# Putting the two halves of an adaLN modulation block into different column quarters of the array

## The chip, the cores and the metric

One core of one Trainium2 chip runs the whole step in one launch. The metric is the device time of the core in microseconds; the kernel before has a median of 1109.49 us over three runs (1108.55 to 1110.03).

Engines in the profile: PE is the matrix engine, PEld its weight loads, DVE the vector engine, ACT the scalar engine, POOL the GpSimd engine, SP the queue that issues the transfers.

## The reference, cut to what matters

Two layers act on 640 tokens of width 1024. Each layer normalizes its input, shifts and scales it by values made from a conditioning vector (adaLN), runs one mixer (a conformer convolution in layer 0, a bidirectional Mamba-2 SSD scan in layer 1), and adds the result, multiplied by a gate. What the change touches is this:

```python
def adaln_params(cond, w, b):
    m = jax.nn.silu(cond) @ w + b          # cond: width 1024, w: 1024 x 3072
    return jnp.split(m, 3, axis=-1)        # shift, scale, gate
...
u = h @ w_in + b_in                        # conformer branch of layer 0
a, a_gate, z = jnp.split(u, 3, axis=-1)
v = a * jax.nn.sigmoid(a_gate)
v = depthwise_conv(v, w_dw, b_dw)          # 31 taps
v = jax.nn.silu(layer_norm(v, ln_g, ln_b))
return (v * jax.nn.silu(z)) @ w_out
```

There are two conditions, one for the 128 context tokens and one for the 512 sample tokens, so each product with `w` has only two rows that count.

## The kernel before, in words

**The big products.** Activations lie with channels on the partitions and tokens along the free axis. A weight comes by DMA as f32 (`wf`), ACT casts its high part to fp32r (`wh`), and DVE or POOL subtracts to get the low part (`wl`). A product is then three: `h_hi` with `wh`, `h_hi` with `wl`, `h_lo` with `wh` (`dense`, L148, and `product`, L499). The trace shows these as 128x320 products.

**The modulation blocks.** 3072 columns of two layers make 24 blocks of 256 columns; the two halves of a block are 128 columns each, for instance shift and scale of one channel tile. For a block, `ada_products` multiplies the conditions (`scz[:, k, :]`, 128 x 32, two columns that count) with eight weight tiles of 128 x 256. The stationary operand is 32 columns wide, so the four column quarters of the array hold four weight tiles at a time: tile k goes to quarter k % 4, and the result in PSUM has four groups of 32 rows that must still be added. `row` is a copy of that to SBUF (ACT). `ada_turn` multiplies it by a constant of zeros and ones, `sel`, which adds the quarters and turns the result so that channels lie on partitions: one product for each half. `ada_bias` (DVE, L129) adds the bias and writes `mod`. In the trace one f32 product has two weight loads and two product records.

**Where the blocks run.** Eight blocks stand at the start (`ada(k)`), between norm of the input, its modulation (`h_hi` and `h_lo`, L214 and L219) and the first products of layer 0, `u`. A tile scheduler orders them there by its own costs. Twelve stand in the loop of layer 0, one in each of twelve channel tiles: `lead` (L582) puts the sixteen products ahead of the gate tile's own product, `after_g` (L516) copies the row, the turn stands behind the tile of `a` (L596), and `after_a` adds the bias. The order in this loop comes from a planner that is given costs in us with each step: `op(ACT, 0.36, ...)` for the row copy, `op(PE, 0.25, ...)` for the turn. Four more blocks stand ahead of layer 1 (`gates`), again ordered by the tile scheduler. These use PSUM named `ada`; in the loop the rows lie in spare columns of the `u` tiles.

**The rest of layer 0.** The depthwise convolution runs on DVE (`cva`, L633, one instruction a tap) and, for other taps, on ACT (`tp`, L664) with POOL adding (`cv`, L705). Then comes a norm over channels: sums on PE (`pst`, `pmr`), then for each of sixteen tiles `cn` minus mean (L805), times the reciprocal (L806), silu on ACT (L807), and times `sz` (L811) on DVE. ACT and POOL make `y_hi` and `y_lo` of it, and PE multiplies with `w_out` into the `o` tiles (L148), whose low weight parts `wl` (L80) are made on DVE between the norm's instructions.

Of the kernel before, what the change touches and what calls it, by code (L numbers as in the profile page):

```python
# [7 lines left out]
F32 = mybir.dt.float32  # L8
# [5 lines left out]
P = 128  # L14
NT = 640
NP = 128
HN = 320
KD = 8
# [8 lines left out]
_n = 0  # L27
for _name, _w in (
    ("ng0", 8), ("ng1", 8), ("fg", 8), ("ada_b", 48), ("cond", 16), ("w_c", 24 * 5), ("b_c", 24),
    ("sn_g", 16), ("dtb", 1), ("alog", 1), ("sel", 2), ("eye", 128), ("d", 32),  # L30
):
    _C[_name] = (_n, _n + _w)
    _n += _w
# [8 lines left out]
def trunk(ctx: ExitStack, tc: tile.TileContext, a: dict):  # L42
# [5 lines left out]
    V, S, G, T = nc.vector, nc.scalar, nc.gpsimd, nc.tensor  # L48
# [6 lines left out]
    def c(name, i=0, n=1):  # L55
        o = _C[name][0] + i
        if o >= NCST:
            return cst0[0][:, o - NCST : o - NCST + n]
        return cst[:, o : o + n]

    eye = c("eye", 0, 128)
# [45 lines left out]

    def ada_products(ws, ps, busy=None):
        for k, w in enumerate(ws):
            q = k % 4 * 32  # L110
            T.matmul(ps[q : q + 32, 0:256], lhsT=scz[:, k, :], rhs=w, start=k < 4, stop=k >= 4)
            if busy is not None and k % 4 == 3:

                for b in range(2):
                    T.matmul(busy[:, b, 0:256], lhsT=w[:, 0:128], rhs=w, start=True, stop=True)
        row = ap.tile([P, 256], F32, tag="ada_row", bufs=2, name="ada_row")
        S.copy(out=row, in_=ps[:, 0:256])
        return row

    def ada_turn(row, ps):  # L120
        for j in range(2):
            T.matmul(ps[:, 2 * j : 2 * j + 2], lhsT=row[:, j * 128 : j * 128 + 128], rhs=c("sel", 0, 2), start=True, stop=True)

    def ada_bias(l, b, ps, act=False):
        if act:
# [109 lines left out]
    PE, ACT, VE, PO, SP, VL = range(6)  # L235
# [95 lines left out]
    def op(eng, dur, fn, table=None):  # L331
        return "op", ((eng, dur, fn, table),)
# [71 lines left out]
    with tc.tile_pool(name="l0", bufs=1) as lp:  # L404
# [102 lines left out]
        def after_g(i, ps, n=None):  # L507

            yield get("tm")
            sgs[i] = tmp.tile([P, NT], F32, tag="tm", bufs=2, name="sg")  # L510
            t = yield op(ACT, 0.79, lambda: S.activation(out=halves(sgs[i]), in_=ps[:, :, 0:HN], func=AF.Sigmoid, bias=c("b_in", 16 + i)), "sig")
            post(("sg", i), t)
            if n is not None:
                l, b, ws = rows_[n][0]
                r = ap.tile([P, 256], F32, tag="ada_row", bufs=2, name="ada_row")
                t = yield op(ACT, 0.36, lambda: S.copy(out=r.rearrange("p (b n) -> p b n", b=2), in_=ps[:, :, HN : HN + 128]))  # L516
                rows_[n] = l, b, r
                post(("row", n), t)
            if i != 1:
                put("mm", t)  # L520
# [48 lines left out]
        def filler():  # L569
            for name in plan:  # L570
                i = int(name[1:])
                n = i - 2 if 2 <= i < 14 else None
                if name[0] == "g":
                    lead = None
                    if n is not None:
                        yield key(("wa", n))

                        def lead(ps):
                            for k, w in enumerate(rows_[n][0][2]):
                                q = k % 4 * 32  # L580
                                for b in range(2):
                                    T.matmul(ps[q : q + 32, b, HN : HN + 128], lhsT=scz[:, k, :], rhs=w[:, b * 128 : b * 128 + 128], start=k < 4, stop=k >= 4)  # L582
                    ps, t = yield from product(16 + i, lead)
                    if n is not None:
                        for _ in range(4):
                            put("cs", t)
                        post(("ada", n), t)
                    start(after_g(i, ps, n), t)
                elif name[0] == "z":
                    ps, t = yield from product(32 + i)  # L590
                    start(after_z(i, ps), t)
                else:
                    ps, t = yield from product(i)
                    if n is not None:
                        yield key(("row", n))
                        t = yield op(PE, 0.25, lambda: ada_turn(rows_[n][2], ps[:, 0, 480:484]))  # L596
                    j = i - 6 if i >= 6 else None
                    if j is not None:
                        yield key(("sq", j))

                        def sums():
                            for t_, b in ((cv[j], 0), (sgs["sq", j], 1)):
                                quarter_sums(ps[:, b, HN : HN + QN], t_, True, True)
                        t = yield op(PE, 0.78, sums)
                        put("tm", t)
                    start(after_a(i, ps, n, j), t)
# [1139 lines left out]
def layout(inp):  # L1746

    import numpy as np

    f = {k: np.asarray(v) for k, v in inp.items()}  # L1750
    con = np.ascontiguousarray
    z = {}
    xa = np.concatenate([f["x_prompt"].reshape(2, 64, 1024), f["x_sample"].reshape(2, 256, 1024)], axis=1)
    z["x"] = con(xa.reshape(NT, KD, P).transpose(2, 1, 0))
    blocks = [(k, 8 + k) for k in range(8)] + [(16 + 2 * k, 17 + 2 * k) for k in range(4)]
    wa = f["ada_w"].reshape(2, KD, P, 24, 128)
    z["w_ada"] = con(np.stack([wa[:, :, :, list(b)] for b in blocks], axis=1).transpose(0, 1, 3, 2, 4, 5)).reshape(24, P, 2048)
    z["w_in1"] = con(f["conv_w_in"][0].reshape(KD, P, 48, 128).transpose(2, 1, 0, 3)).reshape(48, P, 1024)
    wo = f["conv_w_out"][0].reshape(8, 2, P, 1024)
    for i, (m0, nm) in enumerate(((0, 2), (2, 4), (6, 2))):  # L1760
        z[f"w_out1_{i}"] = con(wo[:, :, :, m0 * 128 : (m0 + nm) * 128].transpose(0, 2, 1, 3)).reshape(8, P, 2 * nm * 128)
    wi = f["ssd_w_in"][0]
    z["w_xbc"] = con(wi[:, 2048:5120].reshape(KD, P, 24, 128).transpose(2, 1, 0, 3)).reshape(24, P, 1024)
    z["w_z"] = con(wi[:, 0:2048].reshape(KD, P, 16, 128).transpose(2, 1, 0, 3)).reshape(16, P, 1024)

    def rows4(v):

        return np.concatenate([v[0:32], v[0:32], v[32:64], v[32:64]])

    wd = rows4(wi[:, 5120:5184].T).T.reshape(KD, P, 128)  # L1770
    z["w_dt"] = con(wd.transpose(1, 0, 2)).reshape(P, 1024)
    z["w_out2"] = con(f["ssd_w_out"][0].reshape(4, 4, P, 4, 256).transpose(0, 3, 2, 1, 4)).reshape(4, 4, P, 1024)
    for k, n in (("st_f", "state_fwd"), ("st_b", "state_bwd")):
        z[k] = con(f[n][0, 0].reshape(NG, 8, 64, 128).transpose(0, 3, 1, 2)).reshape(NG, P, 512)
    cs = np.zeros((P, NCST + NCST0), np.float32)

    def put(name, arr):
        lo, hi = _C[name]
        cs[: arr.shape[0], lo:hi] = arr

    def cols(v):
        return v.reshape(-1, P).T

    put("ng0", cols(f["norm_g"][0]))
    put("ng1", cols(f["norm_g"][1]))
    put("fg", cols(f["final_norm_g"]))
    put("b_in", cols(f["conv_b_in"][0]))
    put("w_dw", f["conv_w_dw"][0].reshape(CK, 16, P).transpose(2, 1, 0).reshape(P, 16 * CK))
    put("b_dw", cols(f["conv_b_dw"][0]))
    put("ln_g", cols(f["conv_ln_g"][0]))  # L1790
    put("ln_b", cols(f["conv_ln_b"][0]))
    put("ada_b", np.stack([f["ada_b"].reshape(2, 24, P)[:, list(b)] for b in blocks], axis=1).reshape(48, P).T)
    put("cond", np.stack([f["c_ctx"].reshape(KD, P).T, f["c"][0].reshape(KD, P).T], axis=-1).reshape(P, 16))
    put("w_c", f["ssd_w_conv"][0].reshape(5, 24, P).transpose(2, 1, 0).reshape(P, 120))
    put("b_c", cols(f["ssd_b_conv"][0]))
    put("sn_g", cols(f["ssd_norm_g"][0]))
    put("dtb", rows4(np.concatenate([f["ssd_dt_bias_f"][0], f["ssd_dt_bias_b"][0]]))[:, None])
    put("alog", rows4(np.concatenate([f["ssd_a_log_f"][0], f["ssd_a_log_b"][0]]))[:, None])
    sel = np.zeros((P, 2), np.float32)
    for q in range(0, P, 32):  # L1800
        sel[q, 0] = sel[q + 1, 1] = 1.0
    put("sel", sel)
    put("eye", np.eye(P, dtype=np.float32))
    put("d", np.broadcast_to(f["ssd_d"][0][None, :], (P, NH)))
    z["cst"] = cs
    lower = np.tril(np.ones((64, 64), np.int32), -1)
    z["msk"] = np.concatenate([lower, 1 - lower])
    return z
# [33 lines left out]
```

## Time and profile before

| what | value |
|---|---|
| median of the runs | 1109.49 us |
| lowest and highest run | 1108.55 and 1110.03 us |
| span of the profiled execution | 1108.6 us |
| PE busy | 1064.6 us (96%) |
| DVE busy | 815.5 us (74%) |
| ACT busy | 593.3 us (54%) |
| POOL busy | 521.2 us (47%) |

The span is that of one execution, and the median lies 0.9 us above it. The busy time of PE is modelled from its instruction stream. The modulation products of the start and of the stage ahead of layer 1 have line L111 (192 product records for 12 blocks), those of the loop L582 (384 records for 12 blocks), the turns L122, the row copies L117 and L516. Roughly, 0 to 64 us is the start, 64 to 316 the loop, 393 to 460 the norm with the first `o` products, 460 to 549 the other `o` products, 549 to 560 the stage ahead of layer 1, and the rest is layer 1.

### The profile page before, as it was taken

The numbers are of one execution on the slowest core, as the hardware profiler recorded it, in microseconds if no ns is written. First come the engines' busy times: TensorE is split into PE (matmuls) and PEld (weight loads), VectorE is DVE, ScalarE is ACT, GpSimd is POOL, SyncE is SP. The second block draws the span as 40 slices with busy tenths as digits, with TensorE's granted clock in tenths as the row PEclk, the third lists the DMA queues.
The fourth block names the chain that finished last, engine by engine and source line by source line (L and its number), as shares of the span: only waits on it lengthen the run. The fifth ranks groups of instructions, "written<-read, shape, count | busy, mean of one in ns | idle before, by whom it ended". The sixth has DMA issues, their size and how long they took to land.

```text
span 1108.6 us, 19536 instructions
## 1 busy us (share of the span) xinstructions
PE 1064.6 (96%) x7752; PEld 983.9 (89%) x7752; DVE 815.5 (74%) x1156; ACT 593.3 (54%) x1021; POOL 521.2 (47%) x447
## 2 busy tenths in 40 slices
PE   6999899999988999899999999999999999999996
PEld 3899899999987999899999887899889888978896
DVE  2589989999888479413369878988775786767673
ACT  6646565656665466312267657594536473743442
POOL 1059998988999647200000065413541443244213
PEclk9999999999989999899999999999999999999997
DMA  9364244332112111523402373424342514343102
GB/s 360 152 210 134 78 133 134 121 128 76 59 58 77 58 39 38 184 73 95 137 8 96 97 165 105 102 81 124 90 111 95 115 59 113 106 122 97 40 20 95
DMA packets 79051, 115.98 MB, mean 105 GB/s; under 512 B 26096, under 2 KB 49008, under 8 KB 78960
## 3 DMA queue, kind: packets, MB, share of 16 engines
q1 hardware_dynamic: 78240, 113.91, 34.3%
q8 instruction: 61, 1.00, 0.4%
q10 hardware_dynamic: 720, 0.82, 0.2%
q14 instruction: 30, 0.25, 0.1%
HBM read 109.80 MB, written 4.92 MB: 103 GB/s over the span
## 4 chain that ended last, share of the span: by engine, by line
PE 56%; DVE 21%; POOL 11%; ACT 5%; issue 4%; DMA 2%; SPq 0%; POOLq 0%; DVEq 0%; ACTq 0%
DVE cva L633 9%; PE pz L1004 8%; PE o L1004 8%; POOL cv L705 6%; PE xs L1004 6%; PE o L1513 3%; PE po L1285 2%; POOL wl L480 2%; PE pst L1222 2%; DVE cn L805 2%; PE B L1004 2%; PE py L1353 2%; DVE xs L1046 2%; PE o__5063 L148 1%; PE o__5065 L148 1%
## 5 line engine op out<-in xcount | busy, mean ns | idle before, releaser
L633 DVE SCALAR_TENSOR_TENSOR cva<-v,cst,cva 128x570 f32<-128x570 f32 (+10 forms) x359 | 276.2, 819 | 15.8 <-ACT cva L625 11.6
L705 POOL TENSOR_TENSOR cv<-cv,tp 128x490 f32<-128x490 f32 (+5 forms) x121 | 144.6, 1195 | 8.1
L664 ACT ACTIVATE tp<-v,cst 128x490 f32<-128x490 f32 (+5 forms) x121 | 85.6, 722 | 83.5 <-POOL cv L705 83.3
L966 ACT CAST wh<-wf 128x1024 fp32r<-128x1024 f32 x53 | 55.5, 1047 | 84.8 <-PE xs L1004 21.2
L480 POOL TENSOR_TENSOR wl<-wf,wh 128x1024 fp32r<-128x1024 f32 x37 | 89.0, 2405 | 14.6 <-ACT wh L477 11.0
L1004 PE MATMUL o<-yhl,wh 128*128 128x320 f32 x384 | 92.1, 327 | 0.0
L970 DVE TENSOR_TENSOR wl<-wf,wh 128x1024 fp32r<-128x1024 f32 x51 | 67.1, 1316 | 33.4 <-ACT wh L966 32.2
L1004 PE MATMUL pz<-h_hi,wh 128*128 128x384 f32 (+1 forms) x256 | 84.6, 330 | 0.5 <-ACT up L1033 0.5
L1291 POOL TENSOR_TENSOR y<-y,yo 128x512 f32<-128x512 f32 x32 | 44.6, 1395 | 79.8 <-DVE yo L1289 79.7
L1004 PE MATMUL pz<-h_hi,wl 128*128 128x384 f32 (+1 forms) x256 | 79.1, 309 | 0.0
L1004 PE MATMUL pz<-h_lo,wh 128*128 128x384 f32 (+1 forms) x256 | 79.0, 309 | 0.0
L1004 PE MATMUL xs<-h_hi,wh 128*128 128x384 f32 (+1 forms) x224 | 77.5, 346 | 0.0
L80 DVE TENSOR_TENSOR wl<-wf,wh 128x512 fp32r<-128x512 f32 (+1 forms) x25 | 26.3, 1054 | 69.3 <-ACT wh L78 69.3
L78 ACT CAST wh<-wf 128x1024 fp32r<-128x1024 f32 (+1 forms) x37 | 31.8, 860 | 83.9 <-PE o__5066 L148 39.2
L1004 PEld LDWEIGHTS o<-yhl,wh 128*128 128x128 f32 x384 | 63.9, 188 | 7.8 <-issue 7.8
L1046 DVE SCALAR_TENSOR_TENSOR xs<-up,cst,xs 128x642 f32<-128x642 f32 x64 | 68.3, 1069 | 2.6 <-ACT xs L1044 1.2
L1004 PE MATMUL xs<-h_hi,wl 128*128 128x384 f32 (+1 forms) x224 | 69.2, 309 | 0.0
L1004 PE MATMUL xs<-h_lo,wh 128*128 128x384 f32 (+1 forms) x224 | 69.1, 309 | 0.0
L1160 POOL TENSOR_TENSOR gb<-gb,cols 128x512 f32<-128x512 f32 x20 | 25.4, 1270 | 77.2 <-DMA gb<-acd 77.1
L1004 PE MATMUL o<-yhl,wl 128*128 128x320 f32 x192 | 59.2, 309 | 0.0
L1166 ACT ACTIVATE gf<-gf,cols 128x128 f32<-128x128 f32 x160 | 49.8, 390 | 16.2 <-DVE gf L1162 16.1
L909 POOL MEMSET up<- 128x2 f32 x2 | 0.2, 100 | 120.6 <-DVE h_lo L219 120.6
(764 smaller groups left out, 3487.1 us busy)
## 6 DMA issues: line engine op xcount, KB each, us to landing
wf<-w_in SPq DMA_DIRECT2D x48, 512.0 KB, 3.6
wa<-w_ada SPq DMA_DIRECT2D x64, 256.0 KB, 4.7
wf<-w_out SPq DMA_DIRECT2D x24, 512.0 KB, 4.0
wf<-w_xbc SPq DMA_DIRECT2D x24, 512.0 KB, 3.7
gf<-acd SPq DMA_DIRECT2D x40, 256.0 KB, 5.4
wa<-w_ada SPq DMA_DIRECT2D x16, 512.0 KB, 10.2
wf<-w_z SPq DMA_DIRECT2D x16, 512.0 KB, 3.9
gb<-acd SPq DMA_DIRECT2D x40, 128.0 KB, 4.6
```

Of the source, the lines that this page charges most:

```text
L78: S.copy(out=wh[:, :n], in_=wf[:, :n])
L480: t = yield either((PO, 2.41, lambda: G.tensor_sub(out=wl, in0=wf, in1=wh.bitcast(F32))), (VL, 1.23, lambda: V.tensor_sub(out=wl, in0=wf, ...
L633: t = yield op(VE, 0.24 + 0.01 * (hi - lo), lambda: V.scalar_tensor_tensor(out=rows64(accs[i], lo, hi), in0=rows64(vs[i], lo + d, hi + d), ...
L664: t = yield op(ACT, 0.72, lambda: S.activation(out=tp[:, :, 0 : hi - lo], in_=rows64(vs[i], lo + d, hi + d), func=AF.Copy, scale=w_dw(i, t ...
L705: t = yield op(PO, 1.12 if i < 14 else 1.3, lambda: G.tensor_add(out=rows64(cv[i], lo, hi), in0=rows64(cv[i], lo, hi), in1=sgs["tp", i, n] ...
L966: S.copy(out=cell["wh"], in_=cell["wf"])
L970: e_.tensor_sub(out=cell["wl"], in0=cell["wf"], in1=cell["wh"].bitcast(F32))
L1004: T.matmul(ps[:, b, at_ : at_ + t1 - t0], lhsT=w_, rhs=t_[:, t0:t1], start=k == 0 and n == 0, stop=k == nk - 1 and n == 2)
L1046: t = yield op(VL, 0.89, lambda: V.scalar_tensor_tensor(out=acc, in0=u[:, d : d + PW], scalar=c("w_c", j * 5 + d), in1=acc, op0=ALU.mult, ...
L1166: t = yield op(ACT, 0.39, lambda: S.activation(out=gv[:, h_, :], in_=gv[:, h_, :], func=AF.Exp, bias=cols1[ch][:, o8 + h_ : o8 + h_ + 1]), ...
L1291: t = yield op(PO, 1.29, lambda: G.tensor_add(out=y, in0=y, in1=yo))
L1513: T.matmul(ps, lhsT=wt, rhs=t_[:, tok], start=k == 0 and n == 0, stop=k == 3 and n == 2)
```

## The change

Half j of weight tile k goes to quarter `64 * j + k % 2 * 32` instead of both halves to quarter `k % 4 * 32`. A block is then sixteen products of 128 moving columns everywhere (in the loop it was that already), its result is 128 rows by 128 columns, the row copy is 128 wide instead of 256, and one turn with a `sel` of four columns takes the place of two turns with two. Two planner costs are lowered accordingly.

```diff
     def ada_products(ws, ps, busy=None):
         for k, w in enumerate(ws):
-            q = k % 4 * 32
-            T.matmul(ps[q : q + 32, 0:256], lhsT=scz[:, k, :], rhs=w, start=k < 4, stop=k >= 4)
+            for j in range(2):
+                q = 64 * j + k % 2 * 32
+                T.matmul(ps[q : q + 32, 0:128], lhsT=scz[:, k, :], rhs=w[:, j * 128 : j * 128 + 128], start=k < 2, stop=k >= KD - 2)
...
-        row = ap.tile([P, 256], F32, tag="ada_row", bufs=2, name="ada_row")
-        S.copy(out=row, in_=ps[:, 0:256])
+        row = ap.tile([P, P], F32, tag="ada_row", bufs=2, name="ada_row")
+        S.copy(out=row, in_=ps[:, 0:128])
         return row
 
     def ada_turn(row, ps):
-        for j in range(2):
-            T.matmul(ps[:, 2 * j : 2 * j + 2], lhsT=row[:, j * 128 : j * 128 + 128], rhs=c("sel", 0, 2), start=True, stop=True)
+        T.matmul(ps, lhsT=row, rhs=c("sel", 0, 4), start=True, stop=True)
...
-                r = ap.tile([P, 256], F32, tag="ada_row", bufs=2, name="ada_row")
-                t = yield op(ACT, 0.36, lambda: S.copy(out=r.rearrange("p (b n) -> p b n", b=2), in_=ps[:, :, HN : HN + 128]))
+                r = ap.tile([P, P], F32, tag="ada_row", bufs=2, name="ada_row")
+                t = yield op(ACT, 0.26, lambda: S.copy(out=r, in_=ps[:, 0, HN : HN + 128]))
...
                             for k, w in enumerate(rows_[n][0][2]):
-                                q = k % 4 * 32
                                 for b in range(2):
-                                    T.matmul(ps[q : q + 32, b, HN : HN + 128], lhsT=scz[:, k, :], rhs=w[:, b * 128 : b * 128 + 128], start=k < 4, stop=k >= 4)
+                                    q = 64 * b + k % 2 * 32
+                                    T.matmul(ps[q : q + 32, 0, HN : HN + 128], lhsT=scz[:, k, :], rhs=w[:, b * 128 : b * 128 + 128], start=k < 2, stop=k >= KD - 2)
...
-                        t = yield op(PE, 0.25, lambda: ada_turn(rows_[n][2], ps[:, 0, 480:484]))
+                        t = yield op(PE, 0.22, lambda: ada_turn(rows_[n][2], ps[:, 0, 480:484]))
...
-    sel = np.zeros((P, 2), np.float32)
+    sel = np.zeros((P, 4), np.float32)
     for q in range(0, P, 32):
-        sel[q, 0] = sel[q + 1, 1] = 1.0
+        for cd in range(2):
+            sel[q + cd, q // 64 * 2 + cd] = 1.0
```

In the loop of layer 0 the rows of PE stand as before, but for the turn, and on DVE, ACT and POOL a few neighbours change places. In the parts that the tile scheduler orders, more moves. On PE in the start, where `u__254` and the like are the first tiles of layer 0, the rows of before between 35 and 38 us of its trace are these (an L111 row of four products is half a block):

```order
L148 MATMUL u__254<-h_hi,wh 128x320
L122 MATMUL ada<-cst,ada_row 128x2 x2
L111 MATMUL ada<-wa,scz 32x256 x4
L148 MATMUL u__253<-h_lo,wh 128x320 x2
L111 MATMUL ada<-wa,scz 32x256 x4
L148 MATMUL u__102<-h_lo,wh 128x320 x2
L148 MATMUL u__254<-h_hi,wh 128x320
L148 MATMUL u__254<-h_hi,wl 128x320 x2
L148 MATMUL u__254<-h_lo,wh 128x320 x2
L111 MATMUL ada<-wa,scz 32x256 x8
```

From the turn at 34.54 us of the trace to the end of the last modulation products of the start, before has five groups of L111 with 4, 4, 8, 12 and 4 products. On PE at the end of that stretch the changed kernel has this (half a block is now eight products):

```order
L148 MATMUL u__274<-h_lo,wh 128x320 x2
L112 MATMUL ada<-wa,scz 32x128 x5
L122 MATMUL ada<-cst,ada_row 128x4
L112 MATMUL ada<-wa,scz 32x128 x3
L148 MATMUL u__102<-h_lo,wh 128x320
L112 MATMUL ada<-wa,scz 32x128 x8
L148 MATMUL u__102<-h_lo,wh 128x320
L148 MATMUL u__275<-h_lo,wh 128x320 x2
```

The same four blocks now stand in ten groups, of 8, 8, 8, 5, 3, 5, 11, 5, 3 and 8 products, and three of the turns stand inside a half block.

On DVE at the end of the norm, where the low weight parts `wl` for `w_out` stand between the norm's tiles, before has this:

```order
L811 TENSOR_TENSOR sz_4474<-cn,sz_4474 128x640
L80 TENSOR_TENSOR wl<-wf,wh 128x512
L805 TENSOR_TENSOR cn<-cv_3678,mu 128x640
L806 TENSOR_TENSOR cn<-cn,rl 128x640
L811 TENSOR_TENSOR sz_4544<-cn,sz_4544 128x640
L80 TENSOR_TENSOR wl<-wf,wh 128x512
L805 TENSOR_TENSOR cn<-cv_3857,mu 128x640
L806 TENSOR_TENSOR cn<-cn,rl 128x640
L811 TENSOR_TENSOR sz_4619<-cn,sz_4619 128x640
L80 TENSOR_TENSOR wl<-wf,wh 128x512
L811 TENSOR_TENSOR sz_4688<-cn,sz_4688 128x640
```

and the changed kernel, on the same engine and for the same tiles, this:

```order
L811 TENSOR_TENSOR sz_4518<-cn,sz_4518 128x640
L805 TENSOR_TENSOR cn<-cv_3722,mu 128x640
L806 TENSOR_TENSOR cn<-cn,rl 128x640
L811 TENSOR_TENSOR sz_4588<-cn,sz_4588 128x640
L80 TENSOR_TENSOR wl<-wf,wh 128x512
L805 TENSOR_TENSOR cn<-cv_3901,mu 128x640
L80 TENSOR_TENSOR wl<-wf,wh 128x512
L806 TENSOR_TENSOR cn<-cn,rl 128x640
L811 TENSOR_TENSOR sz_4663<-cn,sz_4663 128x640
L80 TENSOR_TENSOR wl<-wf,wh 128x512
L811 TENSOR_TENSOR sz_4732<-cn,sz_4732 128x640
```

The first of these three `wl` stands behind three more instructions of the norm than before, and the second stands ahead of two that it followed.

Layer 1 behind the stage of `gates` stands in the same order on every engine, and so do the transfers.

More of the change, by code (lines that the diff above doesn't have):

```diff
@@ L29 @@
     ("ng0", 8), ("ng1", 8), ("fg", 8), ("ada_b", 48), ("cond", 16), ("w_c", 24 * 5), ("b_c", 24),
-    ("sn_g", 16), ("dtb", 1), ("alog", 1), ("sel", 2), ("eye", 128), ("d", 32),
+    ("sn_g", 16), ("dtb", 1), ("alog", 1), ("sel", 4), ("eye", 128), ("d", 32),
 ):
```

## The prediction

> **What bounds the kernel now.** I read the page's busy line and chain first, then busy times by stage, then the chain and the waits inside the stage that holds half of the changed blocks, and last single rows of the weight loads where the changed work stands.
>
> ```profile
> PE 1064.6 (96%) x7752; PEld 983.9 (89%) x7752; DVE 815.5 (74%) x1156; ACT 593.3 (54%) x1021; POOL 521.2 (47%) x447
> PE 56%; DVE 21%; POOL 11%; ACT 5%; issue 4%; DMA 2%; SPq 0%; POOLq 0%; DVEq 0%; ACTq 0%
> ```
>
> PE is busy nearly always, so a saving there looks like time. Yet it holds only 56% of the chain that ended last; where DVE and POOL hold it, PE's saving is worth nothing. The stages tell which is where (columns: busy us and count of PE, PEld, DVE, ACT, POOL, then PE clock, DMA share, GB/s).
>
> ```profile
> 20.00:64.00 44.00, 41.96 (x330) 34.77 (x330) 24.39 (x39) 27.72 (x52) 9.58 (x10) 1.00 0.55 208
> 64.00:120.00 56.00, 56.00 (x459) 55.18 (x458) 55.04 (x78) 29.22 (x46) 44.66 (x37) 1.00 0.45 148
> 120.00:135.00 15.00, 11.62 (x95) 10.94 (x94) 15.00 (x22) 10.12 (x13) 14.29 (x14) 0.89 0.22 71
> 200.00:260.00 60.00, 60.00 (x521) 58.82 (x520) 59.75 (x86) 34.81 (x57) 50.62 (x46) 1.00 0.38 124
> 300.00:330.00 30.00, 25.44 (x169) 24.92 (x168) 24.90 (x32) 18.87 (x30) 28.67 (x26) 0.89 0.23 71
> 460.00:545.00 85.00, 83.37 (x564) 82.07 (x564) 25.93 (x34) 18.97 (x24) 0.00 (x0) 0.98 0.32 100
> ```
>
> From 20 to 64 us DVE is busy for 24 of 44 us and PE for 42: this stage goes at PE's pace. From 64 to 260 PE and DVE are both full, so only waits can tell which leads. From 460 PE leads alone. The chain taken inside 64 to 318 us, and the waits of PE and DVE that matter there:
>
> ```profile
> by line: DVE cva L633 37.7%; POOL cv L705 27.0%; issue 10.3%; POOL wl L480 9.1%; POOL seam L693 4.2%; POOL seam L689 2.3%; DVE v L527 1.9%; ACT tp L664 1.6%; ACT cva L625 1.0%; POOL cv L699 0.9%; ACT wh L477 0.8%; ACT cv L640 0.8%; DVE ssum
> PE u__4054 L157 <- ACT sz L543: 4.9, 1, 4.9
> PE u__3666 L499 <- ACT sg L511: 4.6, 1, 4.6
> PE u__1440 L582 <- ACT sz L543: 3.4, 1, 3.4
> DVE v L527 <- PE u__1539 L122: 2.2, 1, 2.2
> ```
>
> No line of PE is among its leading ones: the convolution's `cva` and `cv` carry that stage. PE is full because it runs ahead, and it pays for that with 3.4, 4.6 and 4.9 us of waiting where buffers run out. DVE waits for PE once, 2.2 us.
>
> **The change, part by part.** *The turn.* These are weight loads on PE in the start (start us, duration, line, count, in brackets idle time before).
>
> ```profile
> 40.68 1.00 PEld L122 LDWEIGHTS ada<-cst,ada_row 128*128 128x128 f32 x8
> 41.61 0.30 PEld L148 LDWEIGHTS u__253<-h_lo,wh 128*128 128x128 f32 x2
> 49.95 0.56 PEld L122 LDWEIGHTS ada<-cst,ada_row 128*128 128x128 f32 x4
> 50.43 0.30 PEld L148 LDWEIGHTS u__253<-h_lo,wh 128*128 128x128 f32 x2
> ```
>
> Two turns with eight loads take 0.93 us from start to next start, one with four takes 0.48, so a load is worth 0.11 and a turn of two loads saves 0.22. That four columns move instead of two I cost at nothing: the load sets the pace.
>
> *The products.* Groups of L111 and of the loop's L582 with what follows each:
>
> ```profile
> 31.20 0.30 PEld L148 LDWEIGHTS u__253<-h_lo,wh 128*128 128x128 f32 x2 [0.58 <-DVE h_lo L219]
> 35.12 0.16 PEld L111 LDWEIGHTS ada<-wa,scz 128*32 128x32 f32 x8
> 36.17 0.16 PEld L111 LDWEIGHTS ada<-wa,scz 128*32 128x32 f32 x8 [0.19 <-issue]
> 36.74 0.30 PEld L148 LDWEIGHTS u__102<-h_lo,wh 128*128 128x128 f32 x2 [0.41 <-issue]
> 37.96 0.59 PEld L111 LDWEIGHTS ada<-wa,scz 128*32 128x32 f32 x16 [0.19 <-issue]
> 38.96 0.30 PEld L148 LDWEIGHTS u__253<-h_hi,wh 128*128 128x128 f32 x2 [0.41 <-issue]
> 64.39 0.85 PEld L582 LDWEIGHTS u__706<-wa,scz 128*32 128x32 f32 x32 [0.19 <-PE u__602 L499]
> 65.44 0.19 PEld L499 LDWEIGHTS u__706<-h_hi,wh 128*128 128x128 f32 x1 [0.20 <-issue]
> ```
>
> Eight records take 0.57 us, sixteen 1.00: 0.43 for half a block, and 0.14 plus the idle 0.19 ahead, 0.33 in all, for having a group at all. Behind a turn (35.12) the 0.19 is missing. In the loop a block with moving width 128 takes 1.05 for 32 records, against 1.00 for 16 with width 256: narrower products cost 0.05 a block, and the four quarters overlap already before. So the new order of quarters gains nothing in itself.
>
> [...]
>
> *The start.* From the wait at 31.20 on PE is full to 64, but for this row, where ACT makes it wait 0.69:
>
> ```profile
> 44.39 0.30 PEld L148 LDWEIGHTS u__253<-h_hi,wh 128*128 128x128 f32 x2 [0.69 <-ACT h_hi L214]
> 28.04 0.30 PEld L148 LDWEIGHTS u__254<-h_hi,wh 128*128 128x128 f32 x2 [1.06 <-ACT wh L78]
> ```
>
> Five turns lie behind 31.20: 5 x 0.22 = 1.1 saved. Four blocks with narrow products: 4 x 0.05 = 0.2 more. The order now has ten groups instead of five: 5 x 0.33 = 1.65 more, less 2 x 0.19 = 0.38 because two more of them stand right behind a turn. Groups of 5, 3, 5, 11, 5, 3 fill the quarters unevenly: 11 rounds of four instead of 8; a round is half of the 0.43 of half a block, so 3 x 0.215 = 0.64 more. Sum +1.0, of which I let the wait at 44.39 take 0.3: **+0.7**. Bounds: -1.1, if groups cost nothing because later waits take them, and +2.1, if the wait takes nothing and one late row copy adds a wait as that at 28.04. Three turns ahead of 31.20 lie in time when ACT and DVE lead (the wait at 28.04, that at 31.20), so I cost them at nothing.
>
> *The row copy.* No copy of 128x128 from a product in four quarters is in the trace; the nearest is the transposed tiles' in layer 1 (busy us, mean ns):
>
> ```profile
> L117 ACT COPY ada_row<-ada 128x256 f32<-128x256 f32 x12 | 4.4, 363 | 3.4 <-PE ada L111 3.0 <-PE ada L122 0.4
> L1072 ACT COPY xt<-ptx 128x128 f32<-128x128 f32 x16 | 4.1, 254 | 4.0 <-PE ptx L1070 4.0
> ```
>
> That is 0.11 less on ACT for each of 24 blocks, 12 of them in the loop, 1.3 us in all there. ACT leads the loop's chain only in pieces (`tp` 1.6%, `cva` 1.0%, `cv` 0.8%), so I take **-0.2** with the next term.
>
> *The loop.* Twelve turns: 12 x 0.22 = 2.65 us less on PE. The cover is the convolution on DVE and POOL; PE just waits longer in the 3.4, 4.6 and 4.9 us. Only the turn of `u__1539`, on which DVE waits 2.2, is on the path, and it is 0.22 of that. The moved neighbours on POOL, DVE and ACT change nothing in work. Bounds: -2.65 if PE does lead, +1.2 if a moved instruction on POOL (a low weight part ahead of a convolution row) delays one row.
>
> *The norm.* Two products that stood ahead of `pst` now follow, 0.3 earlier for the chain. But look at the `wl` that PE waits for (columns as before):
>
> ```profile
> 436.26 0.71 DVE L80 TENSOR_TENSOR wl<-wf,wh 128x512 fp32r<-128x512 f32 x1
> 436.89 2.21 DVE L805 TENSOR_TENSOR cn<-cv,mu 128x640 f32<-128x640 f32 x1
> 440.60 1.97 DVE L80 TENSOR_TENSOR wl<-wf,wh 128x512 fp32r<-128x512 f32 x1
> 446.20 1.97 DVE L80 TENSOR_TENSOR wl<-wf,wh 128x512 fp32r<-128x512 f32 x1
> 437.38 0.46 PE L148 MATMUL o__4818<-y_hi,wl 128*128 128x320 f32 x2
> 442.63 0.56 PE L148 MATMUL o__4818<-y_hi,wl 128*128 128x320 f32 x2 [1.57 <-DVE wl L80]
> 448.23 0.56 PE L148 MATMUL o__4818<-y_hi,wl 128*128 128x320 f32 x2 [1.82 <-DVE wl L80]
> ```
>
> Each `wl` feeds 3.8 us of products (442.63 to 446.41, where the wait of 1.82 starts). The first, ready at 436.97 and used at 437.38, now follows three instructions of the norm (3.7 us, 436.89 to 440.60): ready at 440.7 to 441.9. The second, ahead of two it followed, is ready at 448.17 less 0.74 x 2 less 0.71 to 1.97, so 444.7 to 446.0; products go on to 448.5 to 449.8, and the third is ready at 448.2 as before. PE passes this place 0.3 to 1.6 later, middle 0.9; with the 0.3 earlier **+0.6**, bounds -0.5 and +1.3. Behind it PE leads to 545 and hides nothing.
>
> *Ahead of layer 1.*
>
> ```profile
> 549.58 1.45 PEld L111 LDWEIGHTS ada<-wa,scz 128*32 128x32 f32 x32 [0.19 <-issue]
> 552.52 0.16 PEld L190 LDWEIGHTS rps<-rms_sq,ones 128*32 128x32 f32 x8
> ```
>
> Before, two blocks start at 549.58, one at 553.47, one earlier. Now 13 products stand earlier (three fewer than the 16 of a block, 0.2 less), 19 at this place, and a block of 16 ahead of the sums at 552.52, which it holds by about 0.2; four turns of 0.22 less lie beside ACT and DVE making `h_hi`. **0**, bounds -0.5 and +0.4.
>
> Sum: 0.7 - 0.2 + 0.6 + 0 = +1.1. On the profiled span of 1108.6 that is 1109.7; the median lies 0.9 above the span, hence 1110.6 us. About 0.2%, 2.2 us, is what a measurement of this kernel can tell from no change, and +1.1 lies inside.
>
> **The rivals.** *PE leads throughout.* Its 96% and the full windows speak for it; the loop's chain, without PE, speaks against. Then 12 + 5 turns pass, -3.75, and the split groups go under in waits: 1109.5 - 3.75 = 1105.7. It decides for faster once 2.2 of that pass. Chance 0.2.
>
> *Row copies come late for turns inside groups.* Three turns of the start now stand inside half a block; if the scheduler's costs are optimistic, PE stands at the turn until ACT, busy 28 of 44 us there, has copied the row, with that half block, the `u` products and the first tile's `v` queued behind. For it speaks the 1.06 at 28.04 behind ACT's cast; against, that no turn behind 31.20 waits now. Three such waits are 3.2, on +1.1: 1113.8. It decides for slower once these waits exceed 1.1 together. Chance 0.27.
>
> *It changes nothing.* The quarters overlap already, turns and copies are hidden, and the moved `wl` and groups fall into waits: 1109.5. Chance 0.17.
>
> My forecast itself has 0.36; with the last rival, 0.53 for within 0.2%. 1110.6 is the forecast's time; its own range is 1109.3 to 1111.7. The range to 1106.8 leaves out the fuller half of the PE rival, to 1113.3 the worst of the copies: about 0.1 on each side.
>
> **What the trace after would show.** Turns at 0.26 to 0.27 from start to next start; a block alone near 1.05; row copies near 254 ns. The first `cva` of the loop later by about 0.7, waits of PE in the loop longer by some 2.5 in sum, loop no shorter; PE idle at two `wl` near 441 and 445. I am wrong towards faster if the loop's DVE chain shortens with PE, or if the start ends earlier in spite of ten groups; wrong towards slower if a turn of the start has ACT's copy ahead of it, or if a moved low weight part stops the POOL chain.

## The result, and the profile after

The changed kernel takes 1107.26 us in the median of seven runs (1105.53 to 1107.67) against 1110.03 for seven of the kernel before: a ratio of 0.9969, interval 0.9956 to 0.9982. It is faster by 3.4 us, where I forecast 1.1 slower and gave "faster" 0.2. Run again, it gave 0.9967 (0.9955 to 0.9978).

The page's busy line and chain of the profiled execution (span 1105.5 against 1108.6):

```profile
PE 1057.0 (96%) x7896; PEld 980.5 (89%) x7896; DVE 816.4 (74%) x1156; ACT 590.5 (53%) x1021; POOL 521.1 (47%) x447
PE 56%; DVE 21%; POOL 9%; ACT 6%; issue 4%; DMA 3%; SPq 1%; POOLq 0%; DVEq 0%; ACTq 0%
```

PE has 7.6 us less to do, but its share of the chain is what it was. DMA has 3% of it instead of 2 and SPq 1% instead of 0. The stages after (columns as in the prediction):

```profile
20.00:64.00 44.00, 40.30 (x397) 34.83 (x396) 23.27 (x35) 25.75 (x50) 9.15 (x9) 1.00 0.54 206
300.00:330.00 30.00, 25.05 (x166) 24.52 (x165) 24.87 (x32) 18.88 (x30) 28.67 (x26) 0.89 0.23 71
460.00:545.00 85.00, 84.60 (x595) 84.05 (x594) 26.71 (x37) 18.16 (x23) 0.00 (x0) 1.00 0.33 106
```

From 20 to 64 us PE is busy 1.66 us less and waits that much more; 300 to 330 is as it was. From 460 to 545 the granted clock is 1.00, where it was 0.98. Setting the starts of the same instruction side by side in the two traces shows where the time went (minus is earlier): the first `cva` of the loop +0.46 us, the last `cv` on POOL -0.09, the `pmr` products -0.45, the last `sz` of the norm -1.75, the first residual from the `o` products -2.21, the fifth -3.74, the first `dt` product of layer 1 -3.33. So 3.3 us of the gain arise between 393 and 515 us, in the norm and behind it, where no product, copy or turn of the change stands.

What happens there is told by the chain taken inside 445 to 466 us of before (start us, duration us, what; `...` marks rows left out), from the low weight part `wl` that PE waits for to the first tile of the second part of `w_out`, `o__5063`:

```profile
446.28 1.90 DVE wl L80
...
451.63 1.61 PE o__4819 L148 x6
453.25 0.35 SPq L104
...
453.69 6.65 DMA wf<-w_out
...
460.41 1.05 ACT wh L78
...
461.49 1.24 DVE wl L80
...
462.77 0.94 PE o__5063 L148 x4
```

and in the changed kernel, inside 443 to 464 us, where `o__5107` is that tile:

```profile
445.82 0.61 DVE wl L80
...
446.45 0.33 SPq L76
...
446.82 0.43 SPq L104
...
451.04 7.08 DMA wf<-w_out
...
458.20 1.05 ACT wh L78
...
459.28 1.24 DVE wl L80
...
460.56 0.86 PE o__5107 L148 x4
```

L104 is the load of modulation weights `wa` for layer 1: eight transfers that stand on SP's one queue ahead of the first transfer of the second part of `w_out`. Ahead of them stands the last transfer of the first part, which needs a weight buffer that DVE frees with that `wl`. In the timeline of before and of after:

```profile
448.20 0.33 SPq L76 DMA_DIRECT2D wf<-w_out  x1
448.57 5.03 SPq L104 DMA_DIRECT2D wa<-w_ada  x8
453.69 15.53 SPq L76 DMA_DIRECT2D wf<-w_out  x5
```

```profile
444.38 2.39 SPq L76 DMA_DIRECT2D wf<-w_out  x2
446.82 4.13 SPq L104 DMA_DIRECT2D wa<-w_ada  x8
451.04 11.88 SPq L76 DMA_DIRECT2D wf<-w_out  x4
```

DVE frees it at 446.43 instead of 448.18, the eight take 4.13 instead of 5.03 us (before, one of them waited 1.1 us for PE to release its buffer, behind products that ran at half clock, 0.50 from 449.73 to 453.14), so `w_out` goes out 2.65 us earlier; its transfer takes 0.43 longer, and PE goes on 2.21 earlier. The rest of this pair of executions, 1.5 us, is the clock; it has a part of its own below.

The transfer itself is not steady. In a kernel of the experiments that has the norm's order alone (order_only), `w_out` goes out at 451.62, 2.07 earlier than before, but the chain has this row:

```profile
451.62 8.16 DMA wf<-w_out
```

There the transfer takes 1.51 longer than before, and the first residual comes only 0.55 earlier. So how much of DVE's lead comes through the queue differs between traces, and each trace is one execution.

### The profile page after: what moved, and what is told of

Same layout as the page of the kernel before. It is cut to its first block, busy times and chain, and to the rows that moved or that the text cites. A ratio compares the mean times of both kernels' runs of the same rounds, so it can differ in the third digit from the quotient of the medians.

```text
span 1105.5 us, 19815 instructions
## 1 busy us (share of the span) xinstructions
PE 1057.0 (96%) x7896; PEld 980.5 (89%) x7896; DVE 816.4 (74%) x1156; ACT 590.5 (53%) x1021; POOL 521.1 (47%) x447
## 4 chain that ended last, share of the span: by engine, by line
PE 56%; DVE 21%; POOL 9%; ACT 6%; issue 4%; DMA 3%; SPq 1%; POOLq 0%; DVEq 0%; ACTq 0%
DVE cva L633 9%; PE pz L1004 8%; PE o L1004 8%; PE xs L1004 6%; POOL cv L705 5%; PE o L1513 3%; PE po L1285 2%; PE pst L1222 2%; PE B L1004 2%; DVE cn L805 2%; DVE xs L1046 2%; PE py L1353 2%; POOL wl L480 2%; DVE wl L970 1%; PE C L1004 1%
## 5 line engine op out<-in xcount | busy, mean ns | idle before, releaser
L633 DVE SCALAR_TENSOR_TENSOR cva<-v,cst,cva 128x620 f32<-128x620 f32 (+11 forms) x359 | 276.0, 820 | 15.3 <-ACT cva L625 11.1
```

Source lines behind the costliest of these rows:

```text
L633: t = yield op(VE, 0.24 + 0.01 * (hi - lo), lambda: V.scalar_tensor_tensor(out=rows64(accs[i], lo, hi), in0=rows64(vs[i], lo + d, hi + d), ...
```

## The experiments

**Which part of the change?** Two kernels mix old and new blocks. In the built programs only the start decides the norm's order: with the start rewritten, the `wl` stand as in the changed kernel; with the start left and the loop and `gates` rewritten, as before. First the start alone, as an edit of the kernel before (`ada_products` and `ada_turn` below are the new form, those with `_o` the old):

```diff
     def ada_block(l, b, ws, ps, busy=None):
         ada_turn(ada_products(ws, ps, busy), ps[:, 256:260])
...
-                pgs[-1][1].append((l, b, ada_products(ws, ...)))
+                pgs[-1][1].append((l, b, ada_products_o(ws, ...)))
...
-                        t = yield op(PE, 0.22, lambda: ada_turn(rows_[n][2], ...))
+                        t = yield op(PE, 0.25, lambda: ada_turn_o(rows_[n][2], ...))
```

> The new form of a block only in the start; the loop and the stage ahead of layer 1 as before. The low weight parts in the norm stand in the order of the changed kernel. Theory W (the gain is half-clock windows of 3.41 us, behind PE's waits for low weight parts at 442 to 463 us, that no longer come): 1.7 us for each window that goes, so -1.5 to -3.5 on the kernel before, with no half-clock window between 440 and 470 us. Theory T (the gain is PE's shorter turns): the start's part alone, +0.5, and the windows stay.

Measured: ratio 0.9983 (0.9969 to 0.9997), -1.9 us. Against the expectation, a half-clock window stays, at 441.66 us. Then the start left as it was, and the loop and `gates` in the new form, as an edit of the changed kernel:

```diff
     def ada_block(l, b, ws, ps, busy=None):
-        ada_turn(ada_products(ws, ps, busy), ps[:, 256:260])
+        ada_turn_o(ada_products_o(ws, ps, busy), ps[:, 256:260])
```

> The new form in the loop and ahead of layer 1, the start as before; the low weight parts in the norm stand in the order of before. Theory W: half-clock windows near 450 and 463 us stay, time within 1 us of before. Theory T: 12 turns of 0.22 saved on PE, -2.6 us.

Measured: 1.0005 (0.9993 to 1.0017). In its trace one of the two half-clock windows is left, at 460.98. Twelve turns less on PE, 2.6 us by their sum, give nothing: the rival "PE leads throughout" falls. That the start alone gains, though its products now stand in more groups and no instruction of the norm is edited, points away from the operations.

**The norm's order by itself.** The kernel before, with two `wl` put where the changed kernel has them, by dependencies of order alone:

```diff
+                if kp_ in BEHIND:      # {3: last instruction of tile 13, 4: first of tile 15}
+                    tc.add_manual_dep(subs[-1].ins, todo[BEHIND[kp_]].ins.name, ..., reason="order")
```

> The kernel before, with two of the low weight parts in the norm put, by order alone, where the changed kernel has them; no operation changed. Theory W: PE's waits become about 2.2 and 0.6 instead of 1.57 and 1.82, at least one half-clock window goes: -1.7 to -3.5. Theory T: 0. My prediction's own working: +0.3 to +1.6.

Measured: 0.9979 (0.9967 to 0.9991), -2.3 us with an interval of -3.7 to -1.0 (the medians of all runs, 1108.33 and 1109.57, lie 1.2 apart). And the converse, the changed kernel with the `wl` put back:

```diff
+                if kp_ == 5:           # behind the last instruction of tile 14
+                    tc.add_manual_dep(subs[-1].ins, todo[...].ins.name, ..., reason="order")
+                if kp_ in AHEAD:       # {3: first instruction of tile 14, 4: of tile 15, 5: last of tile 15}
+                    tc.add_manual_dep(todo[AHEAD[kp_]].ins, subs[-1].ins.name, ..., reason="order")
```

> The changed kernel in all its operations, with the low weight parts of the norm put back, by order alone, where the kernel before has them. If the gain is the norm's order: it goes, 0 to +1 us on before. If it is anything in the operations of the change: -3 us stay.

Measured: 0.9995 (0.9985 to 1.0005). All operations of the change without the norm's order gain nothing that can be measured, and the interval lies clear of the changed kernel's; the order without the operations gains a good part of it. These two settle that the norm's order is the cause. What the operations are worth by themselves stays between -1.7 and +0.6 us.

Why is the other order shorter on DVE? From the first `pmr` product to the last `sz`, the traces of six kernels with the old order take 54.95 to 55.09 us, those of six with the new one 53.59 to 53.69: 1.35 us, whatever else differs. In order_only DVE runs as before up to 436 us, so the difference lies behind that. Before, from the timelines of DVE and, last row, POOL (start us, duration us, then engine, line and operands):

```profile
436.89 2.21 DVE L805 TENSOR_TENSOR cn<-cv,mu 128x640 f32<-128x640 f32 x1
439.13 0.83 DVE L806 TENSOR_TENSOR cn<-cn,rl 128x640 f32<-128x640 f32 x1
440.60 1.97 DVE L80 TENSOR_TENSOR wl<-wf,wh 128x512 fp32r<-128x512 f32 x1
442.50 2.20 DVE L805 TENSOR_TENSOR cn<-cv,mu 128x640 f32<-128x640 f32 x1
446.20 1.97 DVE L80 TENSOR_TENSOR wl<-wf,wh 128x512 fp32r<-128x512 f32 x1
436.55 1.85 POOL L815 TENSOR_TENSOR y_lo<-sz,y_hi 128x640 fp32r<-128x640 f32 x1
```

and order_only:

```profile
436.53 0.83 DVE L812 TENSOR_TENSOR cn<-cv,mu 128x640 f32<-128x640 f32 x1
438.87 1.94 DVE L82 TENSOR_TENSOR wl<-wf,wh 128x512 fp32r<-128x512 f32 x1
440.73 2.19 DVE L812 TENSOR_TENSOR cn<-cv,mu 128x640 f32<-128x640 f32 x1
442.84 2.06 DVE L82 TENSOR_TENSOR wl<-wf,wh 128x512 fp32r<-128x512 f32 x1
446.29 0.68 DVE L82 TENSOR_TENSOR wl<-wf,wh 128x512 fp32r<-128x512 f32 x1
```

The same `cn` (L805, in order_only L812) takes 0.83 or 2.2, the same `wl` 0.7 or 2.0, while L806, one of whose inputs lies in PSUM, takes 0.82 or 0.83 in every row of the norm. The long `cn` of before starts inside POOL's instruction that ends at 438.40 and itself ends 0.70 later; each of the long ones here ends 0.55 (`wl`) or 0.7 (`cn`) behind an end on POOL. The norm of before from 395 us on shows the same: seven `cn` of L805 start inside an instruction of POOL, take 1.83 to 2.68 us and end 0.69 behind that instruction's end; the other nine take 0.82 or 0.83. So in these traces a `cn` (L805) or `wl`, both of whose inputs lie in SBUF, that starts while POOL is at work ends 0.55 to 0.7 behind the end of POOL's instruction, as if it waited for that. Of the rows above four are long before and three in order_only, and one long instruction is worth 1.3 to 1.4 us. That the waiting is for POOL I read from these ends; no kernel took POOL's work away, so that part is argued from the rows.

**The queue.** The kernel before, with the eight `wa` transfers behind the seventh transfer of the second part of `w_out`:

```diff
-            if pi != 1:
-                loaded += [ada_load(1, 8 + pi + b, ...) for b in range(2)]
+            if pi == 2:
+                loaded += [ada_load(1, 8 + pi + b, ...) for b in range(2)]
...
+                if (pi, kp) == (1, 5):
+                    loaded += [ada_load(1, 8 + b, ..., wdma[-1]) for b in range(2)]   # order: behind that transfer
```

> The kernel before; eight transfers of modulation weights for layer 1, which stood on SP's queue ahead of the first transfers of the second part of w_out and could not start before the norm's last instruction on DVE, now stand behind the seventh of those. Theory Q (the end of the norm on DVE, through this queue, sets when PE goes on at 461.5): PE's waits there of 1.22 and 0.41 go and with them the half-clock window at 463, -1.6 to -3.3 us. Theory P (PE's own waits for low weight parts at 442 and 448 set it): 0.

Measured: 0.9967 (0.9955 to 0.9980), -3.7 us, with nothing of the change. Of PE's waits between 430 and 470 us the trace has one row left (us in total, times, longest):

```profile
PE o__4802 L152 <- DVE wl L82: 3.4, 2, 1.8
```

The two waits near 442 and 448, on which I had built, are all there; the waits at 461.5 are gone, and the time with them. The changed kernel with the transfers moved:

> The changed kernel with the same transfers moved. Theory Q: waits of 0.84 and 0.40 go, -1.2 us on the changed kernel, about -4.3 on the kernel before. Theory P: as the changed kernel.

Measured: 0.9963 (0.9950 to 0.9976), median 1105.56. That is within the intervals of the changed kernel (0.9967) and of queue_before, so with the queue out of the way the change has no gain that these runs can tell, as it must be if its gain comes through the queue; the -1.2 I expected on top is not confirmed by the times, though the profile has `dt` at 553.60, 1.3 earlier than after.

**Filling the waits.** In the kernel before, products that nothing reads, ahead of those that wait:

```diff
         for n, (w, h) in enumerate(((ws, hi), (wls, hi), (ws, lo))):
+            for m in range(fill if n == 1 else 0):
+                T.matmul(ps[:, m % 2, 320:512], lhsT=hi[:, 0:128], rhs=hi[:, 0:192], start=False, stop=False)
```

> The kernel before, with 10 idle products of 128x192 ahead of each of the two products that wait for low weight parts near 442 and 448 us, and 6 ahead of the one near 462, which nothing reads. Order and operations else as before. Theory W: the waits stay as long, but PE is busy in more than half of each 3.41 us, so no half-clock window comes near 450 and 463: -3.4 us, two times 1.7. Theory T, and a theory that the order of the low weight parts alone saves time: 0 or some tenths slower.

Measured: 1.0006 (0.9992 to 1.0019), and -3.4 was expected: a miss, and the one that led to the queue. In the trace the half-clock window at 450 is gone, yet PE gained nothing by it. Its waits:

```profile
PE o__5083 L150 <- ACT wh L78: 3.7, 1, 3.7
PE o__4818 L150 <- DVE wl L80: 1.2, 2, 0.7
```

What PE saved it waited at 463 for `w_out`, 3.7 us, and the half clock came there, for 6.83 us. With the queue moved as well:

> The kernel before with the transfers moved, and 10 idle products ahead of each of the two that wait near 442 and 448 us, which nothing reads. With the queue out of the way a half-clock window at 450 can no longer hide in the wait at 461: theory W (3.41 us windows at half clock, 1.7 us each, where PE was idle for half of the window before) says 0 to -1.7 on the kernel with moved transfers alone, by how often that window comes there. Without W: 0 or some tenths slower.

Measured: 0.9957 (0.9940 to 0.9974), median 1105.01, the fastest of all, but its interval covers that of queue_before. And the changed kernel, with the transfers moved and its one long wait filled, beside the changed kernel again:

> The changed kernel once more, as the reference for the next. About -3 us on before; by theory W its wait of 2.2 us near 440 brings a half-clock window behind it in some executions and not in others, by where the fixed windows of 3.41 us fall, so runs 1.7 us apart.

> The changed kernel with the eight transfers moved and 14 idle products ahead of the one that waits 2.2 us near 440, which nothing reads. Theory W: no half-clock window between 430 and 470 us, 0 to -1.7 us on the changed kernel with moved transfers, so -5 to -6 on before. Without W: as the kernel with moved transfers, -4.1.

Measured: 0.9967 (0.9955 to 0.9978) and 0.9969 (0.9954 to 0.9983). No window of half clock between 430 and 470 us in the second, and still no gain that the runs can tell: the runs of one kernel spread over 2 to 7 us, and in the traces windows elsewhere come and go.

## Why the prediction was wrong

- *What bounds the loop.* Right. The cover was the convolution, and PE's saving went into its waits:

```profile
PE u__3710 L499 <- ACT sg L511: 5.0, 1, 5.0
PE u__4098 L157 <- ACT sz L543: 4.9, 1, 4.9
PE u__1493 L582 <- ACT sz L543: 4.0, 1, 4.0
PE u__3080 L122 <- ACT ada_row L516: 2.4, 1, 2.4
```

  The three that I named grew by 0.4, 0 and 0.6, and the one at a turn, 0.9 before, by 1.5: 2.5 in sum, against 2.65 saved. The loop ends within 0.3 us of where it did, and start_old shows the same in time.

- *The turn, the products and the copy.* Nearly right in size. Weight loads on PE in the start of the changed kernel:

```profile
33.26 0.34 PEld L122 LDWEIGHTS ada<-cst,ada_row 128*128 128x128 f32 x2
33.52 0.30 PEld L148 LDWEIGHTS u__275<-h_hi,wh 128*128 128x128 f32 x2
38.81 0.35 PEld L112 LDWEIGHTS ada<-wa,scz 128*32 128x32 f32 x10 [0.19 <-issue]
39.37 0.30 PEld L122 LDWEIGHTS ada<-cst,ada_row 128*128 128x128 f32 x2 [0.20 <-issue]
39.68 0.15 PEld L112 LDWEIGHTS ada<-wa,scz 128*32 128x32 f32 x6
40.03 0.19 PEld L148 LDWEIGHTS u__274<-h_hi,wl 128*128 128x128 f32 x1 [0.20 <-issue]
```

  A turn takes 0.26 from start to next start, and 0.31 inside a half block. Such a half block takes 0.56 and 0.35 in place of 0.57, so a split costs 0.39 with the turn's 0.05. Ahead of the turn 0.20 are idle, where my sum had nothing, and behind it the row shows no idle time, as my sum took it. The row copies take 254 ns (L516) and 258 (L118) in the mean, 254 were expected.

- *The start.* +0.7 forecast; the first `cva` came 0.46 later. But the traces begin differently, so it is better counted from the first turn. From there to the first `cva` the six kernels with the old start take 40.78 to 40.80 us, five with the new one 42.05 to 42.07, and the profiled execution of the changed kernel 42.83, where one more wait of 1.2 us, for a transfer of `wa`, stands. So the start costs about 1.3 us, inside my bounds, but by other terms: up to the loop's first modulation product, PE's work grew by 0.3 instead of 1.0, and its idle time, of which I let 0.3 be taken, by 1.0 (2.0 to 3.0), mostly ahead of products that need `h_hi` and `h_lo`. No turn waited for a row copy there long enough to decide for the second rival.

- *The norm.* Here the prediction failed. I had +0.6 for the place where PE passes, and measured -1.75 at the last `sz` on DVE, of which -0.45 is the earlier `pmr` (forecast as -0.3), and -2.21 where PE goes on. One reading of the order was wrong: the second `wl` is not ahead of two instructions that it followed; it stands one later, behind `cn` of the last tile instead of ahead of it, as the edit of order_only has it. It was ready at 444.35, still earlier than the 444.7 to 446.0 that I gave. Two steps of the working were wrong. First, "the third is ready at 448.2 as before": I kept the sum of DVE's work and its long instructions fixed while I moved them. The third `wl` was ready at 446.42, because, as the rows above are read, a long instruction is long by where it meets POOL, and a new order meets it elsewhere. Second, "behind it PE leads to 545 and hides nothing": PE stood 1.22 and 0.41 us at 461.5 for a weight, and the chain from it runs over SP's queue to that same `wl`. The waits of PE at 442 and 448 lie ahead of this one, which hides what is lost or saved there. I took the longest waits of PE by line and did not follow the short one to its transfer, and I looked past the `wa` on SP's queue because the change does not move transfers.

- *Ahead of layer 1.* 0 with bounds to +0.4; it was +0.42 (-3.75 at the last residual, -3.33 at the first `dt`) in this pair of executions, at the upper bound.

- *The level.* I put the median 0.9 above the profiled span; the profiled run of the changed kernel took 1107.31 with a span of 1105.5, so 1.8 lie around it. In the later runs of before the time lies 2.2 above the span of the same run, in those of the changed kernel 1.85. So some 0.4 us of the gain lies outside the spans; no trace shows what it is.

The rivals: PE leading throughout named the right sign for a wrong reason; neither it nor any other rival had a gain that comes from DVE and a queue. The order excerpt on the norm was in my hands, and I read it for PE alone.

## The clock, which I had not expected

In the traces the granted clock falls to half for stretches of 3.41 us or 6.83, two of them in a row, on a fixed grid of 3.41: in before they begin at 128.88, 316.61, 354.16, 449.73, 463.38 and 558.96 us, which lie 55, 11, 28, 4 and 28 such windows apart, and from 1094.84 on it stays at half to the end. Laid on that grid, before has two half-clock windows between 430 and 470 us, each shown here behind the window ahead of it (after the window's length the busy us of PE; the granted clock is third from the end):

```profile
446.31:449.73 3.42, 1.60 (x11) 1.50 (x11) 3.42 (x3) 2.08 (x5) 3.29 (x2) 1.00 0.14 26
449.73:453.14 3.41, 3.41 (x15) 3.41 (x14) 1.11 (x2) 2.04 (x3) 1.55 (x1) 0.50 0.96 291
459.97:463.38 3.41, 1.78 (x11) 1.25 (x10) 1.89 (x3) 2.09 (x2) 0.00 (x0) 1.00 0.06 25
463.38:466.80 3.42, 3.42 (x15) 3.42 (x14) 2.31 (x4) 0.98 (x2) 0.00 (x0) 0.50 0.69 208
```

After, and after once more, at the wait of 2.2 us near 440:

```profile
436.40:439.82 3.42, 1.72 (x12) 1.46 (x10) 3.38 (x4) 2.31 (x4) 3.42 (x3) 1.00 0.00 0
439.82:443.23 3.41, 2.92 (x20) 2.92 (x21) 3.41 (x3) 0.16 (x1) 3.41 (x2) 1.00 0.20 77
```

```profile
438.27:441.69 3.42, 1.48 (x11) 1.22 (x9) 3.38 (x4) 2.06 (x4) 3.42 (x3) 1.00 0.00 0
441.69:445.10 3.41, 3.17 (x12) 3.17 (x13) 3.41 (x3) 0.36 (x1) 3.41 (x2) 0.50 0.25 77
```

A stretch of 3.41 us at half clock costs up to 1.7 us of products, an estimate from half its length; in before a pair of `o` products (128x320) starts every 0.53 us in the window at 449.73 and every 0.29 behind it, which makes it 1.5. Between 430 and 470 us, in the twelve traces, a half-clock window followed each window at full clock in which PE was busy for at most 0.47 of it, one with 0.52 (before, at 459.97), and none with 0.50 (the changed kernel above, and order_only) or with 0.54 and more; ahead of layer 1 one follows a window with 0.65 (before, at 555.54). So the busy time alone does not decide it, and no run shows the half of a window, by which theory W went, as a limit. The wait of 2.2 us near 440, cut otherwise by the grid, left PE busy for 0.50 of a window after, and no half-clock window followed; after once more it left 0.43, and one did.

In the changed kernel's profile both windows are gone. The one at 463 is the 1.5 us that the fifth residual gained on the first. That the wait ahead of it fell from 1.63 to 1.24 us does not explain it: order_only waits 2.65 us there, split over two windows of its grid, and no half-clock window follows:

```profile
456.77:460.18 3.41, 1.94 (x14) 1.68 (x12) 0.00 (x0) 0.32 (x1) 0.00 (x0) 1.00 0.74 302
460.18:463.59 3.41, 2.22 (x13) 1.96 (x14) 2.65 (x4) 2.25 (x3) 0.00 (x0) 1.00 0.15 29
```

So that 1.5 us is in part luck of the executions that were profiled. The granted clocks of all runs bear this out: their mean is 0.9852 for the changed kernel (16 runs) and 0.9846 for before (75 runs), where one window of 3.41 us moves it by 0.0015, by half its length in 1108 us. So the changed kernel has, on average, about 0.4 of a window less, an estimate of 0.7 us; order_only has 0.9844 against 0.9847 of before beside it, and gains all the same. The window at 450 went too, but its 1.7 would mostly have been lost in the wait for `w_out`: in fill_before, which has no such window, `w_out` goes out 60.92 us behind the first `pmr`, in before 60.55.

## What to carry to other kernels

When a change lets a scheduler reorder a later stage, follow each wait of the bound engine there back to its transfer and that transfer to the queue it stood on, short waits too: the time may hang on an instruction far from any that was edited. A saving on PE ahead of such a wait was worth nothing here, and eight transfers moved back on the queue were worth as much as the whole change. Where DVE and POOL shared a stretch here, a DVE instruction with two SBUF inputs, `wl`, took 0.7 or 2.0 us by its place, so its duration can't be carried along when it is moved. And a gain of 3 us in one pair of profiles can hold a half-clock window that the next execution has again: count the windows before reading the rest.
